# Start addresses of SBUF pools: two unused tiles and three tiles rounded up to 512 bytes

## The chip, the cores and the metric

The kernel runs on one core of one Trainium2 chip. The metric is the device time of one execution in microseconds, as the median of several runs. TensorE does the matrix products, VectorE (DVE) and ScalarE (ACT) the element-wise work, GpSimd (POOL) a little of it in the first third, and SyncE (SP) issues nearly all DMA transfers.

## The reference

Two layers of a diffusion backbone over 512 latent tokens of 1024 channels, with 256 context tokens. Layer 0 mixes the tokens with neighbourhood attention and a bidirectional gated recurrence, layer 1 with a gated short convolution; each layer ends in a gated feed-forward stage with a convolution of three taps. All in float32:

```
h = modulate(rms_norm(x, norm_mix_w[l]), shift_m, scale_m)
y = even_mixer(h, h_ctx, ...) if l == 0 else short_conv_mixer(h, ...)
x = x + gate_m * y
h = modulate(rms_norm(x, norm_ffn_w[l]), shift_f, scale_f)
a, val = split(h @ w_up[l])                  # 1024 -> 2 x 2816
x = x + gate_f * ((gelu(dwconv3(a)) * val) @ w_down[l])
...
return rms_norm(x, final_norm_w)
```

The six modulation vectors of a layer are `silu(c) @ ada_w[l] + ada_b[l]`.

## The kernel before

Activations stand transposed, 128 channels in the partitions and 512 tokens in the row. Each float32 operand is split into a high part (rounded to fp32r by a cast on ScalarE) and a low part (the difference, by VectorE), and a product is made of three matmuls, high by high, high by low and low by high: `mm3` (L287 to L290), and L1339 to L1341 in the last projection. The first argument after the output is the stationary operand (128 columns, 512 bytes in a partition), the next one the moving operand (256 or 512 columns).

Where the operands lie:

- `wp` holds the weights: two raw buffers `wraw` that DMAs fill, three pairs `whi`/`wlo` of 4096 bytes each, and `ws3`. In most stages `whi` and `wlo` are the stationary operands. In the value projection (L577) and in the last projection (L1339) they are the moving ones.
- `yp` holds the normalized activations of a stage (h, hf, hm: eight tiles of 4096 bytes, high and low part). They are the moving operands of most projections and the stationary ones of the value projection.
- `gq`, `zp` and `gp` hold the 22 gated feed-forward tiles g (a high and a low part each): g0 to g5 in `gq`, g6 to g9 in `zp`, g10 to g21 in `gp` (`gtiles`, L1216). They are the moving operands of the first down projection (pbd) and the stationary ones of the second (pd). At the ends of projections three weight pairs are put into `gq` too ("spare", L1050).
- `fp` holds the tiles T2 to T4 (sums of quarters of the activations, moving operands in the loop `group`, L1151), the results R and t of that loop, and small tiles, `ss` (L1333) among them.
- `np_` holds the attention tiles. The scores (L870) are made of QS (stationary) and KS (moving).
- `ap_` holds the rows of `ada_w` and their sums, and `ared` (L507).
- `xp` holds the residual stream xT.

The feed-forward stage takes most of the time: one `quad` (four output tiles of 128 channels, matmuls of 256 columns) and ten rounds of `group`, with matmuls of 256 columns on quarters of the product (p<-hf, p<-T) and of 512 columns on the rest (p<-hf). The stages follow each other in the written order; weights are loaded and split some calls ahead (`Weights.ahead`, L130).

Pools are stacked. Those of the left side begin where the one before them ends, from low addresses upward, in the order in which they are entered: cp, wp, ap_, zp, yp, and after them mp and later gp; kvp, hp and np_ come and go above. Those of the right side (xp, fp, gq) are stacked from the end of the partition downward. Every tile is rounded up to 32 bytes. So the size of a small tile in one pool sets where every later pool of its side begins.

Of the kernel before, what the change touches and what calls it, by code (L numbers as in the profile page):

```python
# [9 lines left out]
F32 = mybir.dt.float32  # L10
# [4 lines left out]
ALU = mybir.AluOpType  # L15
AX = mybir.AxisListType
PSUM = bass.MemoryType.PSUM

P = 128
# [155 lines left out]
def backbone(ctx: ExitStack, tc: tile.TileContext, a, out, dump=None):  # L175
    nc = tc.nc
    V, S, G, TE = nc.vector, nc.scalar, nc.gpsimd, nc.tensor
# [12 lines left out]
    cp = ctx.enter_context(tc.tile_pool(name="cp", bufs=1))  # L190
    wp = ctx.enter_context(tc.tile_pool(name="wp", bufs=2))
    ap_ = ctx.enter_context(tc.tile_pool(name="ap_", bufs=1))
# [52 lines left out]
    ident, sel = cst[:, 0:128], cst[:, 128:256]  # L245
# [11 lines left out]
    oml = cp.tile([P, 8], F32, name="oml")  # L257
    noml = cp.tile([P, 8], F32, name="noml")
    amul = cp.tile([P, 5, KT], F32, name="amul")
    rowv = lambda i, n: pv[:, i : i + n]  # L260


# [211 lines left out]
    class Ada:  # L474
# [3 lines left out]
        n, calls, raw, late = 0, 0, {}, []  # L478
# [9 lines left out]
        def unit(self, aux):  # L488
            self.calls += 1
            while self.late and self.late[0][0] <= self.calls:  # L490
                self.late.pop(0)[1]()
            if self.n >= 8 * len(self.jobs):
                return
            r = self.n % 8
            l, p_, j = self.jobs[self.n // 8]
            while len(self.raw) < min(self.n + 3, 8 * len(self.jobs)):
                self.load()
            raw = self.raw[self.n]
            self.n += 1
            if r == 0:  # L500
                self.acc = ap_.tile([P, T], F32, tag="aacc", name=f"aa{self.n}", bufs=1)
                pin(V.tensor_scalar(self.acc[:], raw[:], sil[:, 0, 0:1], None, ALU.mult))
                return
            pin(V.scalar_tensor_tensor(self.acc[:], raw[:], sil[:, r, 0:1], self.acc[:], ALU.mult, ALU.add))  # L504
            if r < 7:
                return
            red = ap_.tile([P, 16], F32, tag="ared", name=f"ad{self.n}", bufs=1)  # L507
            V.tensor_reduce(red[:], self.acc[:].rearrange("p (b j) -> p b j", j=32), axis=AX.X, op=ALU.add,
                            apply_transpose=True)
            pm = []  # L510

            def gather():
                pm.append(aux(f"pad{l}{p_}{j}"))
                TE.matmul(pm[0][:, 0:16], sel, red[:], start=True, stop=True)

            def finish():
                c = p_ * 8 + 4 * j
                for qd in range(4):
                    s4 = slice(32 * qd, 32 * qd + 32)
                    V.tensor_tensor(mod[s4, l, c : c + 4], pm[0][s4, qd:16:4], abT[s4, l * 48 + c : l * 48 + c + 4],  # L520
                                    ALU.add)
                if p_ in (1, 4):
                    w0 = (16 if p_ == 1 else 32) + 8 * l + 4 * j
                    V.scalar_tensor_tensor(amul[:, 2 * l + (1 if p_ == 1 else 2), 4 * j : 4 * j + 4], mod[:, l, c : c + 4],
                                           1.0, pv[:, w0 : w0 + 4], ALU.add, ALU.mult)

            self.late += [(self.calls + 3, gather), (self.calls + 5, finish)]

    ada = Ada()
# [440 lines left out]
                wv.tick()  # L970


    xp = ctx.enter_context(tc.tile_pool(name="xp", bufs=1, side="right", reuse_waits="tile"))
    xT = [xp.tile([P, T], F32, name=f"xT{k}") for k in range(KT)]
    for k in range(KT):
        nc.sync.dma_start(xT[k][:], x[k * P : (k + 1) * P, :])
    fp = ctx.enter_context(tc.tile_pool(name="fp", bufs=1, side="right", reuse_waits="tile"))
# [349 lines left out]
    for i in range(4):  # L1327
        for k2 in range(2):
# [1 line left out]
            for k in range(4):  # L1330
                TE.transpose(pt[:, k * P : (k + 1) * P], xT[4 * k2 + k][:, i * P : (i + 1) * P], ident)
            S.copy(xk[i][:, k2 * T : (k2 + 1) * T], pt[:])
    ss = fp.tile([P, 4, 8], F32, tag="ss", name="ssf")  # L1333

    def down(o, w, i, k0):
        ts = slice(i * P, (i + 1) * P)
# [91 lines left out]
```

## Time and profile before

| | |
|---|---|
| median of 3 runs | 1334.43 us (1333.52 to 1336.91) |
| the profiled execution | 1333.99 us, its span 1332.2 us |
| granted clock of TensorE, mean | 0.995 |
| TensorE matmul busy | 1304.5 us, 8456 matmuls |
| VectorE, ScalarE busy | 965.4 us, 625.2 us |
| bytes moved | 172.35 MB, mean 129 GB/s |

In the rows of the timeline the first number is the start in us from the beginning of the span, the second the duration of the row, then engine, line, operation, output and inputs by their names in the program, and how many instructions the row merges. In the rows of the groups the numbers behind the bar are the busy time in us and the mean duration in ns of one, then the idle time of the engine just before them with what ended it. In the rows of the waits they are us in total, times, and the longest. In a row of the windows the numbers are the stretch, its length, and the busy time and count of instructions of PE, PEld, DVE, ACT and POOL.

### The profile page before, as it was taken

To read this page: it belongs to the slowest core of one execution; us is meant where nothing else is said; L and a number is where in the kernel's file an instruction comes from. 1 tells how busy PE (TensorE), PEld (TensorE's weight loads), DVE (VectorE), ACT (ScalarE), POOL (GpSimd) and SP (SyncE) were. 2 spreads that over 40 slices of the span, in tenths; PEclk is the share of its full clock that TensorE was granted. 3 is DMA by queue.
4 is the path that set the end of the run, shared out by engine and by line. 5 is a ranking of instruction groups with operands and counts; after the bars stand their busy time and mean duration, and the time that the engine had idled before them with its cause. 6 is when DMAs were issued, how large, how long until landed. Compare 5 with 4: busy or idle time off the path is not lost. (4 is left out here: it accounts for less than half of the span.)

```text
span 1332.2 us, 21229 instructions
## 1 busy us (share of the span) xinstructions
PE 1304.5 (98%) x8456; PEld 1147.6 (86%) x8456; DVE 965.4 (72%) x1688; ACT 625.2 (47%) x1085; POOL 84.3 (6%) x87
## 2 busy tenths in 40 slices
PE   7999999999999999999999999999999999999997
PEld 4798888888779998889877898888999989899997
DVE  4668897887778878788766776667789897782333
ACT  4443445555545656565422253223456565663223
POOL 2204332311000000000000000000000000000000
PEclk9999999999999999999999999999999999999999
DMA  9842113674562122323466734555403423242231
GB/s 293 265 123 84 33 33 82 152 182 134 153 206 96 64 99 92 127 71 119 141 211 198 226 132 143 167 165 174 158 27 117 142 80 127 80 146 69 91 108 64
DMA packets 134995, 172.35 MB, mean 129 GB/s; under 512 B 14320, under 2 KB 103792, under 8 KB 129776
## 3 DMA queue, kind: packets, MB, share of 16 engines
q1 hardware_dynamic: 132896, 166.15, 39.3%
q10 hardware_dynamic: 2000, 4.85, 1.4%
q8 instruction: 66, 1.08, 0.3%
q14 instruction: 33, 0.27, 0.1%
HBM read 165.21 MB, written 2.10 MB: 126 GB/s over the span
## 5 line engine op out<-in xcount | busy, mean ns | idle before, releaser
L92 ACT CAST whi<-wraw 128x1024 fp32r<-128x1024 f32 (+1 forms) x122 | 124.1, 1021 | 280.8 <-PE pd L1340 70.4
L93 DVE TENSOR_TENSOR wlo<-wraw,whi 128x1024 fp32r<-128x1024 f32 (+1 forms) x122 | 145.2, 1192 | 107.7 <-ACT whi L92 107.1
L288 PE MATMUL p<-hf,whi 128*128 128x512 f32 (+1 forms) x640 | 215.4, 338 | 1.4 <-ACT whi L125 1.4
L290 PE MATMUL p<-hf,wlo 128*128 128x512 f32 (+1 forms) x640 | 214.6, 335 | 0.0
L289 PE MATMUL p<-hf,whi 128*128 128x512 f32 (+1 forms) x640 | 214.1, 335 | 0.0
L125 ACT CAST whi<-wraw 128x512 fp32r<-128x512 f32 (+1 forms) x160 | 113.0, 727 | 85.0 <-PE p L289 35.0
L290 PEld LDWEIGHTS p<-hf,wlo 128*128 128x128 f32 x640 | 120.1, 188 | 13.6
L288 PEld LDWEIGHTS p<-hf,whi 128*128 128x128 f32 x640 | 120.1, 188 | 12.3 <-ACT whi L125 1.6
L289 PEld LDWEIGHTS p<-hf,whi 128*128 128x128 f32 x640 | 120.1, 188 | 10.7
L126 DVE TENSOR_TENSOR wlo<-wraw,whi 128x512 fp32r<-128x512 f32 (+1 forms) x160 | 128.1, 817 | 0.9 <-ACT whi L125 0.5
L504 DVE SCALAR_TENSOR_TENSOR aa<-ar,sil,aa 128x512 f32<-128x512 f32 x140 | 104.8, 749 | 24.1 <-DMA ar<-in_ada_w_dram 21.8
L1339 PE MATMUL pd<-whi,g 128*128 128x256 f32 x352 | 98.2, 279 | 0.0
L1341 PE MATMUL pd<-wlo,g 128*128 128x256 f32 x352 | 98.1, 279 | 0.0
L1340 PE MATMUL pd<-whi,g 128*128 128x256 f32 x352 | 97.9, 278 | 0.0
L288 PE MATMUL pbd<-g,whi 128*128 128x512 f32 (+1 forms) x192 | 73.5, 383 | 0.0
L289 PE MATMUL pbd<-g,whi 128*128 128x512 f32 (+1 forms) x192 | 73.3, 382 | 0.0
L290 PE MATMUL pbd<-g,wlo 128*128 128x512 f32 (+1 forms) x192 | 73.1, 381 | 0.0
L288 PE MATMUL p<-T,whi 128*128 128x256 f32 x240 | 69.0, 288 | 0.0
L290 PE MATMUL p<-T,wlo 128*128 128x256 f32 x240 | 67.2, 280 | 0.0
L289 PE MATMUL p<-T,whi 128*128 128x256 f32 x240 | 67.2, 280 | 0.0
L1340 PEld LDWEIGHTS pd<-whi,g 128*128 128x128 f32 x352 | 66.3, 188 | 0.0
L1339 PEld LDWEIGHTS pd<-whi,g 128*128 128x128 f32 x352 | 66.1, 188 | 0.0
(679 smaller groups left out, 3296.3 us busy)
## 6 DMA issues: line engine op xcount, KB each, us to landing
ar<-in_ada_w_dram SPq DMA_DIRECT2D x160, 256.0 KB, 3.1
wraw<-in_upq_dram SPq DMA_DIRECT2D x40, 1024.0 KB, 4.8
wraw<-in_ffn_w_down_dram SPq DMA_DIRECT2D x16, 1024.0 KB, 5.3
wraw<-in_od_w_in_dram SPq DMA_DIRECT2D x12, 1024.0 KB, 5.6
wraw<-in_ev_w_in_dram SPq DMA_DIRECT2D x20, 512.0 KB, 5.2
araw<-in_ada_w_dram SPq DMA_DIRECT2D x16, 512.0 KB, 6.3
wraw<-in_ffn_w_down_dram SPq DMA_DIRECT2D x8, 768.0 KB, 4.7
wraw<-in_ev_w_out_dram SPq DMA_DIRECT2D x4, 1024.0 KB, 6.9
```

The costliest lines, as they stand in the source:

```text
L92: self.nc.scalar.copy(hv, rv)
L93: self.pin(self.nc.vector.tensor_tensor(lv, rv, hv.bitcast(F32), ALU.subtract))
L125: self.nc.scalar.copy(hi, src)
L126: V.tensor_tensor(lo, src, hi.bitcast(F32), ALU.subtract)
L288: TE.matmul(o, wh, mh, start=start, stop=False, skip_group_check=True)
L289: TE.matmul(o, wh, ml, start=False, stop=False, skip_group_check=True)
L290: TE.matmul(o, wl, mh, start=False, stop=stop, skip_group_check=True)
L504: pin(V.scalar_tensor_tensor(self.acc[:], raw[:], sil[:, r, 0:1], self.acc[:], ALU.mult, ALU.add))
L1339: TE.matmul(o[i][:, 0:256], gh[:, ts], w[0][:, k - k0], start=k == 0, stop=False)
L1340: TE.matmul(o[i][:, 0:256], gl[:, ts], w[0][:, k - k0], start=False, stop=False)
L1341: TE.matmul(o[i][:, 0:256], gh[:, ts], w[1][:, k - k0], start=False, stop=k == FT - 1)
```

## The change

Two tiles that nothing reads or writes are added, and three small tiles are made larger:

```diff
+    cp.tile([P, 144], F32, name="even")
...
-            red = ap_.tile([P, 16], F32, tag="ared", name=f"ad{self.n}", bufs=1)
-            V.tensor_reduce(red[:], self.acc[:].rearrange("p (b j) -> p b j", j=32), axis=AX.X, op=ALU.add,
+            red = ap_.tile([P, P], F32, tag="ared", name=f"ad{self.n}", bufs=1)[:, 0:16]
+            V.tensor_reduce(red, self.acc[:].rearrange("p (b j) -> p b j", j=32), axis=AX.X, op=ALU.add,
                             apply_transpose=True)
...
-                TE.matmul(pm[0][:, 0:16], sel, red[:], start=True, stop=True)
+                TE.matmul(pm[0][:, 0:16], sel, red, start=True, stop=True)
...
+    ep = ctx.enter_context(tc.tile_pool(name="ep", bufs=1, side="right"))
+    ep.tile([P, 120], F32, name="even2")
     xp = ctx.enter_context(tc.tile_pool(name="xp", bufs=1, side="right", reuse_waits="tile"))
...
-    ss = fp.tile([P, 4, 8], F32, tag="ss", name="ssf")
+    ss = fp.tile([P, P], F32, tag="ss", name="ssf")[:, 0:32].rearrange("p (i n) -> p i n", n=8)
```

The unused tile in `cp` has 576 bytes a partition and fills that pool up to a multiple of 512; the one in the new pool `ep`, 480 bytes, lies between `xp` and the right end of the partition. `ared` grows from 64 to 512 bytes and `ss` from 128 to 512. What follows for the first byte of each pool in a partition, from the allocation of the two built programs:

| pool | before | modulo 512 | now | modulo 512 |
|---|---|---|---|---|
| wp | 9152 | 448 | 9728 | 0 |
| ap_ | 52160 | 448 | 52736 | 0 |
| zp | 60416 | 0 | 61440 | 0 |
| yp | 76800 | 0 | 77824 | 0 |
| mp, gp | 109568 | 0 | 110592 | 0 |
| hp, np_ | 150528 | 0 | 151552 | 0 |
| gq | 160608 | 352 | 159744 | 0 |
| fp | 185184 | 352 | 184320 | 0 |
| xp | 212960 | 480 | 212480 | 0 |

The tiles of wp, gq, fp (T, R, t) and xp are multiples of 512 bytes long, and the slices of 128 columns that become stationary are 512 bytes long, so within these pools all operands of matmuls share the start of the pool modulo 512. KS and QS lie at 0 modulo 512 before and now. The weights of the very first projection (w0h, w0l) lie at 96 before and now. All instructions, their order on each engine and what they wait for are the same in both programs.

## The prediction

> **What bounds the kernel now.** I read the page first: the span, the busy shares, the slices.
>
> ```profile
> span 1332.2 us, 21229 instructions
> ...
> PE 1304.5 (98%) x8456; PEld 1147.6 (86%) x8456; DVE 965.4 (72%) x1688; ACT 625.2 (47%) x1085; POOL 84.3 (6%) x87
> ...
> PE   7999999999999999999999999999999999999997
> ...
> PEclk9999999999999999999999999999999999999999
> ```
>
> TensorE is busy in 98% of the span and in 9 tenths or more of every slice but the first and the last, at the full granted clock throughout. No other engine comes near. The waits say the same from the other side:
>
> ```profile
> PE prx L412 <- ACT sqx L410: 5.1, 1, 5.1
> ...
> PE p L288 <- ACT whi L125: 1.4, 2, 0.7
> ...
> ACT whi L92 <- PE pd L1340: 70.4, 18, 4.8
> ```
>
> The longest wait of TensorE for anybody is 5.1 us, once, at the start (L412); in the whole feed-forward loop (L288) it waits 1.4 us. ScalarE waits 70.4 us for TensorE, because a weight buffer comes free only when the last matmul that reads it is done. So the time is the number of matmuls times the step from one matmul's start to the next, and a change that adds no work can act only through this step. These groups hold most of the matmuls (each of them is one of a triple of lines with equal counts):
>
> ```profile
> L288 PE MATMUL p<-hf,whi 128*128 128x512 f32 x320 | 125.7, 393 | 0.0
> L1339 PE MATMUL pd<-whi,g 128*128 128x256 f32 x352 | 98.2, 279 | 0.0
> L288 PE MATMUL p<-hf,whi 128*128 128x256 f32 x320 | 90.1, 283 | 1.4 <-ACT whi L125 1.4
> L288 PE MATMUL p<-T,whi 128*128 128x256 f32 x240 | 69.0, 288 | 0.0
> L288 PE MATMUL pbd<-g,whi 128*128 128x512 f32 x160 | 64.3, 402 | 0.0
> ```
>
> The mean durations (279 to 402 ns) overlap, so they are not the step. The step is read in the timeline, from the starts of the first and the last matmul of an undisturbed run and the number of steps between them.
>
> **The step depends on where operands start.** Each matmul has a stationary operand, loaded while the matmul before it streams, and a moving operand. I write m/s for their start bytes modulo 512, m of the matmul that streams and s of the weights being loaded beside it, as the allocation of the built program gives them. First the last stage (L1339 to L1341), where one line, one shape and one set of moving tiles (m 448) meets stationary tiles of two pools: g6 to g21 at 0, then g0 to g5 at 352.
>
> ```profile
> 1275.18 0.28 PE L1339 MATMUL pd<-whi,g 128*128 128x256 f32 x1
> ...
> 1293.88 0.28 PE L1339 MATMUL pd<-whi,g 128*128 128x256 f32 x1
> ...
> 1295.17 0.28 PE L1341 MATMUL pd<-wlo,g 128*128 128x256 f32 x1
> ...
> 1300.21 0.28 PE L1341 MATMUL pd<-wlo,g 128*128 128x256 f32 x1
> ```
>
> 448/0: 165 steps in 18.70 us, 113.3 ns each. 448/352: 42 steps in 5.04 us, 120.0 ns. The same instructions on the same engine, 6.7 ns apart, so the start byte matters. The other classes with 256 columns, hf against whi (0/448) and T against whi (352/448), and one more of 0/448 in the first projection of the feed-forward stage:
>
> ```profile
> 463.15 0.28 PE L288 MATMUL p<-hf,whi 128*128 128x256 f32 x1
> ...
> 465.98 0.28 PE L288 MATMUL p<-hf,whi 128*128 128x256 f32 x1
> ```
>
> ```profile
> 453.19 0.28 PE L289 MATMUL p<-T,whi 128*128 128x256 f32 x1
> ...
> 454.00 0.28 PE L290 MATMUL p<-T,wlo 128*128 128x256 f32 x1
> ```
>
> ```profile
> 422.01 0.28 PE L289 MATMUL ppa<-hf,whi 128*128 128x256 f32 x1
> ...
> 422.46 0.28 PE L290 MATMUL ppa<-hf,wlo 128*128 128x256 f32 x1
> ```
>
> These are 24 steps of 117.8 ns, 7 of 117.1 and 4 of 113.3. The 0/448 class has two rhythms, 113.3 and about 117.8; over the dense part it averages 116.8. With 512 columns (0/448, then 352/448, then 0/96 in the first projection):
>
> ```profile
> 818.25 0.39 PE L288 MATMUL ppc<-hm,whi 128*128 128x512 f32 x1
> ...
> 849.84 0.39 PE L288 MATMUL ppb<-hm,whi 128*128 128x512 f32 x1
> ```
>
> ```profile
> 652.92 0.40 PE L290 MATMUL pbd<-g,wlo 128*128 128x512 f32 x1
> ...
> 660.42 0.40 PE L289 MATMUL pbd<-g,whi 128*128 128x512 f32 x1
> ```
>
> ```profile
> 61.58 0.40 PE L290 MATMUL pq<-h,w0l 128*128 128x512 f32 x1
> ...
> 64.86 0.40 PE L289 MATMUL pq<-h,w0h 128*128 128x512 f32 x1
> ```
>
> 138 steps of 228.9 ns, 32 of 234.3, 14 of 234.3. The last two share neither start; they share the difference s minus m, which is 96 in both. That is my first reason to think that the distance of the two streams counts, and not each start by itself.
>
> **What the change makes.** It adds, removes and moves no instruction: on every engine the built program has the same instructions in the same order with the same waits, SP's and POOL's queues included. It moves starts: weights (wp) from 448 to 0, g0 to g5 and spare weights (gq) and the T tiles (fp) from 352 to 0; the tiles at 0 stay at 0. So nearly every matmul becomes 0/0. The kernel has this class already in one place, the attention scores, KS against QS, both at 0:
>
> ```profile
> 276.85 1.00 PE L870 MATMUL ps<-KS,QS 128*128 128x256 f32 x7
> ```
>
> ```profile
> 313.96 1.00 PE L870 MATMUL ps<-KS,QS 128*128 128x256 f32 x7
> ```
>
> ```profile
> 242.05 0.40 PE L290 MATMUL pk<-h,wlo 128*128 128x512 f32 x1
> 242.28 0.28 PE L870 MATMUL ps<-KS,QS 128*128 128x256 f32 x1
> ```
>
> In the first two rows seven matmuls take 1.00 us with the last one's 0.28 us: 6 steps in 0.72 us, 120 ns, as slow as 448/352 though both operands are on 512. The last two rows are a 512-wide matmul at 0 beside which the first QS at 0 is loaded: 236 ns to the next start, where the three steps before it are 230, 231 and 226. There are seven such places, 231 to 236 ns.
>
> So I take 120 ns for 256 columns at 0/0. Its bounds are 113.3 ns (the best class) and 125 ns (the longest single step in the score rows). For 512 columns the bounds are 226.6 ns (twice 113.3) and 236; I take 232.5, halfway between the 229 of 0/448 and 236, since a single place is no steady run.
>
> After 418 us, where TensorE has no waits worth naming, the classes count as follows (matmuls, mean step now, to which step, sum). 256 columns: 0/448 1342 from 116.8 to 120, +4.3 us; 352/448 720 from 117.7, +1.7; 0/352 382 from 117.5, +1.0; 448/0 768 from 113.4, +5.1; 448/352 276 at 120.0, 0. 512 columns: 0/448 1907 from 229.1 to 232.5, +6.5; 352/448 143 from 234.1, -0.2. Sum +18.4 us, all on the path. Before 418 us the same sum is +5.3 us (604 of 512 columns, 745 of 256; the 128 of 0/96 keep their starts), but there TensorE does wait:
>
> ```profile
> 100.00:200.00 100.00, 96.30 (x730) 83.52 (x730) 88.93 (x150) 43.85 (x73) 36.56 (x38) 1.00 0.18 49
> ```
>
> With 3.7 us idle and VectorE at 88.9 in this stretch, I count half, +2.6 us. The other engines gain or lose nothing by their starts:
>
> ```profile
> L284 ACT CAST T<-df x6: 620/622/624, 435.8 to 982.2; 128x512 fp32r<-128x512 f32 x6
> ...
> L284 ACT CAST mgh<-gg x4: 607/616/622, 156.7 to 367.9; 128x512 fp32r<-128x512 f32 x4
> ```
>
> ```profile
> L285 DVE TENSOR_TENSOR T<-df,T x6: 676/690/693, 436.7 to 982.9; 128x512 fp32r<-128x512 f32 x6
> ...
> L285 DVE TENSOR_TENSOR mgl<-gg,mgh x4: 682/688/693, 175.4 to 368.5; 128x512 fp32r<-128x512 f32 x4
> ```
>
> T lies at 352 and mgh, mgl, gg at 0: 622 against 616 ns, 690 against 688. The ared and ss tiles, rounded up, feed 20 small reductions and the last four scalings; they are read and written in the same shapes, so I cost them at nothing. DMAs land at new starts (wraw from 448 to 0). No row has a landing with the start alone changed; they run beside TensorE, except in the first 45 us, and I leave them at zero.
>
> Sum: the profiled execution took 1333.99 us (span 1332.2); plus 18.4 and 2.6 is 1355.0. Its distance to the median of 1334.43 is 0.4 us, which is nothing here.
>
> **The rivals.** First, each start counts by itself, and 0 is the best for weights. For it: 113.3 against 120.0 in the last stage, where only the stationary tile's start differs, and the steadiness of 448/0 over 165 steps. Against it: KS and QS, both at 0, at 120 ns; and 0/448 at 113.3 in the first projection, where weights at 448 cost nothing. By it all go to 113.3 and 226.6. In the order above the dense classes give -4.7, -3.2, -1.6, -0.1, -1.8, -4.8 and -1.1, sum -17.3 us; before 418 us half of -3.3. That is 1315 us: faster. It decides if a weight load at 0 beside a moving operand at 0 runs at 113.3 in the group loop (L1151), where most of the matmuls are.
>
> Second, no change: the step is set by the rhythm in which matmuls follow each other, as the two rhythms of 0/448 suggest, and the classes trade gains (gq, T) for losses (448/0): 1334 us, give or take 4. The Trainium skill stands on this side. "SBUF — State Buffer", section "Who interferes with whom", gives the PE two independent SBUF read ports, one for the moving operand and one for weight loads, and says that PE never waits on anyone. Its section "Specifications (TRN2)" gives lines of 16 bytes and a penalty for crossing into a new one; all starts here are multiples of 32, before and after. By both sections the change would do nothing, and the time would stay at 1334 us. The trace speaks against it: 113.3 and 120.0 ns for one line and one shape.
>
> **How the numbers follow.** Slower as worked out, 0.56: two separate places of class 0/0 (KS with QS, and h with QS) are slow, and equal differences gave equal steps. Its own range is 1345 (512 columns stay at 229, and some of the 256 keep 117.8) to 1366 (512 columns at 236, early part counted in full). Faster, 0.32: the clean pair in the last stage is the best controlled row there is, and score runs are at most 8 matmuls long. No change, 0.12. A measurement of this kernel tells about 0.3%, 4 us, from nothing. The range goes from 1315, the full gain of the first rival, to 1366, and leaves out some 15 in 100: gains above that sum, and losses above the bounds.
>
> **What would show it.** In the changed kernel the timeline of the last stage, between about 1290 and 1310 us, would show steps of 120 ns for all g tiles, with the break between g5 and g6 gone; 113.3 there would make the first rival right, and the forecast's +5.1 us wrong first. The group loop's 256-wide triples would go to 120, the 512-wide runs to 230 or more; steps of 226.6 there would make the forecast wrong by twice the term. The granted clock and the idle time of TensorE should stay. If the steps are as now in all three places, the second rival holds.

## The result and the profile after

The changed kernel took **1342.53 us** (median of 4 runs, 1340.81 to 1344.33), the kernel before 1334.18 (4 runs): a ratio of 1.0059, with a 95% interval of 1.0039 to 1.0079. It is slower, as forecast, by 8 us where 21 were forecast. Both profiled executions are compared below: 1342.5 us of span against 1332.2. The profiled run of the changed kernel is the slowest of its four, so the traces differ by 10.3 us and the medians by 8.4. All times compared here are of executions at a granted clock of 0.99 or more; one of the twelve of T384_g352 below ran at 0.654, took 1828.86 us and is left out.

The page of the changed kernel, its span, busy times and the clock in 40 slices:

```profile
span 1342.5 us, 21229 instructions
...
PE 1314.5 (98%) x8456; PEld 1162.0 (87%) x8456; DVE 964.6 (72%) x1688; ACT 625.0 (47%) x1085; POOL 84.2 (6%) x87
...
PEclk8999999999999999999998999999999999999999
```

TensorE is busy 10.0 us longer with as many matmuls; VectorE and ScalarE have the times they had (965.4 and 625.2 before). So the loss is in the step of the matmuls, as the prediction had it. Three matmuls that both programs have in the same place of the sequence divide it. The timeline before (start, duration, engine, line, operation), then after:

```profile
407.82 0.28 PE L290 MATMUL pbo<-mgh,wlo 128*128 128x256 f32 x1
...
1208.12 0.28 PE L1340 MATMUL pd<-whi,g 128*128 128x256 f32 x1
...
1324.85 0.28 PE L1341 MATMUL pd<-wlo,g 128*128 128x256 f32 x1
```

```profile
410.40 0.28 PE L291 MATMUL pbo<-mgh,wlo 128*128 128x256 f32 x1
...
1213.79 0.28 PE L1343 MATMUL pd<-whi,g 128*128 128x256 f32 x1
...
1335.58 0.28 PE L1344 MATMUL pd<-wlo,g 128*128 128x256 f32 x1
```

The changed kernel is 2.6 us late at the first, 5.7 at the second and 10.7 at the third:

| stretch | forecast, us | measured, us |
|---|---|---|
| up to 408 | +2.6 | +2.6 |
| 408 to 1208 | +13.3 (256 columns +7.0, 512 columns +6.3) | +3.1 (256 columns +5.6, 512 columns -3.6, the rest +1.1) |
| last stage | +5.1 | +5.1 |

The last column sums the steps of the same matmul in both traces by class, from 418 us on (the ten before add nothing); the rest are some 200 steps longer than 140 ns (256 columns) or 260 ns (512 columns) in one of the traces, which hold a wait or a dip of the clock. That the first row agrees is luck. The prediction had taken half of a sum of +5.3 us, of which its 604 matmuls of 512 columns at +3.4 ns are +2.1 (an estimate from its own numbers) and those of 256 columns the other +3.2. By class the traces have +2.9 with 256 columns, nearly the whole, and -0.3 with 512. The steps are read as in the prediction, from first and last starts. The last stage and a run of T in the group loop, both 256 columns, in the changed kernel:

```profile
1290.10 0.28 PE L1343 MATMUL pd<-whi,g 128*128 128x256 f32 x1
...
1293.94 0.28 PE L1342 MATMUL pd<-whi,g 128*128 128x256 f32 x1
```

```profile
456.74 0.28 PE L291 MATMUL p<-T,wlo 128*128 128x256 f32 x1
...
460.70 0.28 PE L291 MATMUL p<-T,wlo 128*128 128x256 f32 x1
```

32 steps in 3.84 us and 33 in 3.96: 120.0 ns in both, the value taken for 0/0. Now a long run of 512 columns:

```profile
823.10 0.39 PE L291 MATMUL ppc<-hm,wlo 128*128 128x512 f32 x1
...
854.83 0.39 PE L290 MATMUL ppb<-hm,whi 128*128 128x512 f32 x1
```

140 steps in 31.73 us: 226.7 ns, where 232.5 was taken, and less than the 228.9 of 0/448 before. With 512 columns the new starts are the better ones: over all steps from 418 to 1208 us that are not longer than 260 ns the mean went from 229.4 to 227.7 ns.

### The profile page after: what moved, and what is told of

Read it like the earlier page. It is cut to its first block, busy times and chain, and to the rows that moved or that the text cites. A ratio compares the mean times of both kernels' runs of the same rounds, so it can differ in the third digit from the quotient of the medians.

```text
span 1342.5 us, 21229 instructions
## 1 busy us (share of the span) xinstructions
PE 1314.5 (98%) x8456; PEld 1162.0 (87%) x8456; DVE 964.6 (72%) x1688; ACT 625.0 (47%) x1085; POOL 84.2 (6%) x87
## 4 chain that ended last, share of the span: by engine, by line
PE 85%; DVE 8%; ACT 3%; DMA 2%; issue 1%; SPq 0%; ACTq 0%; DVEq 0%
PE p L289 11%; PE p L290 10%; PE p L291 10%; PE pd L1342 3%; PE pd L1344 3%; PE pd L1343 3%; PE pbo L289 2%; PE pbo L291 2%; PE pbo L290 2%; PE pbd L291 2%; PE pbd L289 2%; PE pbd L290 2%; DMA ar<-in_ada_w_dram 2%; PE ppc L289 1%; PE ppc L291 1%; PE ppc L290 1%
## 5 line engine op out<-in xcount | busy, mean ns | idle before, releaser
L290 PEld LDWEIGHTS p<-hf,whi 128*128 128x128 f32 x640 | 121.5, 190 | 10.3
L1342 PE MATMUL pd<-whi,g 128*128 128x256 f32 x352 | 100.0, 284 | 0.0
L1343 PE MATMUL pd<-whi,g 128*128 128x256 f32 x352 | 99.9, 284 | 0.0
L1343 PEld LDWEIGHTS pd<-whi,g 128*128 128x128 f32 x352 | 67.6, 192 | 0.0
L1342 PEld LDWEIGHTS pd<-whi,g 128*128 128x128 f32 x352 | 67.6, 192 | 0.0
```

Of the source, the lines that this page charges most:

```text
L290: TE.matmul(o, wh, ml, start=False, stop=False, skip_group_check=True)
L1342: TE.matmul(o[i][:, 0:256], gh[:, ts], w[0][:, k - k0], start=k == 0, stop=False)
L1343: TE.matmul(o[i][:, 0:256], gl[:, ts], w[0][:, k - k0], start=False, stop=False)
```

## The experiments

**The steps by themselves.** Two kernels measure nothing but the step, on 16 moving and 16 stationary tiles; 16 matmuls of each pair in a row, all pairs twice. Their body in place of the whole computation (512 in place of 256 in the second):

```diff
+    for r, (i, j) in enumerate(runs):
+        x, w, p = ms[offs[i]], ws[offs[j]], o[r % 8]
+        for k in range(16):
+            TE.matmul(p[:, 0:256], w[:, 128 * (k % 4) : 128 * (k % 4) + 128], x[:, 256 * (k % 2) : 256 * (k % 2) + 256],
+                      start=k == 0, stop=k == 15)
```

> This kernel leaves the whole computation out: it zeroes sixteen moving tiles (ma to mp, starting at 0, 32, ... 480 modulo 512) and sixteen stationary tiles (wa to wp, the same starts), and runs each of the 256 pairs twice as 16 matmuls with 256 columns in a row, in two different orders. Theory A, the step depends on the distance s minus m alone: equal steps along every diagonal, near 120 ns for distance 0, 113.3 for 64, 117 to 118 for 96, 352 and 448, 120 for 416, whatever the starts. Theory B, each start counts by itself: the table splits into rows or columns, for instance every moving tile at 448 (mo) at 113.3 or every moving tile at 0 (ma) at 117 to 120 whatever the weights. Theory C, the rhythm with which a run is entered decides: the two passes of one pair differ by several ns, without order in the table.

> The same kernel with 512 columns; the computation is left out here too. Theory A: equal steps along diagonals: 226.7 ns for distance 0, about 229 for 448, 234 for 96. Theory B: rows or columns, moving tiles at 352 slow (234), at 0 fast with weights at 0 (226.7) and slow with weights at 96 (234). Theory C: the two passes differ, 226.7 in one and 231 to 236 in the other for the same pair.

Here the timeline joins a run into one row; its duration less that of the last matmul (0.28 or 0.39 us) over 15 is the mean step. With 256 columns (ma, me, mh, mi, mo start at 0, 128, 224, 256, 448, and so do the w tiles):

```profile
162.57 2.08 PE L204 MATMUL og<-mo,wo 128*128 128x256 f32 x16
...
264.57 2.08 PE L204 MATMUL oe<-me,we 128*128 128x256 f32 x16
...
272.12 2.08 PE L204 MATMUL oa<-mi,wa 128*128 128x256 f32 x16
...
464.77 2.01 PE L204 MATMUL og<-mo,wa 128*128 128x256 f32 x16
...
481.77 2.05 PE L204 MATMUL oh<-mh,wa 128*128 128x256 f32 x16
...
828.26 2.05 PE L204 MATMUL og<-mo,wa 128*128 128x256 f32 x16
```

Three pairs with other starts but a distance of 0 or 256 all take 120 ns a step. The pair 448/0 (mo, wa) takes 115 ns the first time and 118 the second. With 512 columns (mc at 64, wi at 256, wl at 352, wo at 448):

```profile
149.64 3.83 PE L204 MATMUL oc<-mc,wa 128*128 128x512 f32 x16
...
379.80 3.83 PE L204 MATMUL oa<-ma,wo 128*128 128x512 f32 x16
...
498.62 3.81 PE L204 MATMUL oa<-ma,wi 128*128 128x512 f32 x16
...
513.40 3.82 PE L204 MATMUL oe<-me,we 128*128 128x512 f32 x16
...
914.18 3.90 PE L204 MATMUL oa<-ma,wl 128*128 128x512 f32 x16
```

Distance 192 (64/0 and 0/448) and distance 0 take 228 to 229 ns, distance 96 takes 234. From the last twelve steps of each run, by the distance s minus m modulo 256 (medians of the two passes):

| distance | 256 columns, ns | 512 columns, ns |
|---|---|---|
| 0 | 120.1, 120.0 | 228.4, 228.4 |
| 32 | 117.9, 118.1 | 233.2, 232.8 |
| 64 | 113.8, 117.8 | 233.7, 233.3 |
| 96 | 117.1, 118.3 | 234.4, 234.3 |
| 128 | 118.3, 118.9 | 232.6, 233.0 |
| 160 | 120.0, 120.0 | 233.7, 233.3 |
| 192 | 117.8, 117.8 | 228.9, 228.9 |
| 224 | 117.8, 116.7 | 233.3, 233.3 |

Theory A holds: pairs of one distance agree within 2 ns in a pass, whatever their starts, except at 64 and 256 columns, where two values occur (113.3 to 113.8, and 117.8), at 96 and 256 columns (117.1 to 120.0), and for the first runs of a kernel (one with 512 columns, two with 256), where the steps are still 427 and 213 ns. The 228.4 of distance 0 is no settled step: in the second pass the fourth to the seventh step of such a run are some 236, 228, 233 and 231 ns, and the last eight 226 to 227. The distance counts modulo 256, not 512. Theory B falls: there is no good row or column. Theory C holds in so far as one pair of distance 64 takes either value, and in small part one of 96. But the class before is not what decides. In the second pass sixteen runs of distance 64 follow each other, so that all but the first come after the same class:

```profile
561.83 2.05 PE L204 MATMUL ob<-mb,wl 128*128 128x256 f32 x16
563.71 2.05 PE L204 MATMUL oc<-mc,wm 128*128 128x256 f32 x16
565.60 2.00 PE L204 MATMUL od<-md,wn 128*128 128x256 f32 x16
567.44 2.05 PE L204 MATMUL oe<-me,wo 128*128 128x256 f32 x16
569.33 2.05 PE L204 MATMUL of<-mf,wp 128*128 128x256 f32 x16
571.22 2.00 PE L204 MATMUL og<-mg,wa 128*128 128x256 f32 x16
```

Every third run settles at 113.3 ns and the two between at 117.8, in both such rows of sixteen. An order of this kind looks like a phase that is carried from run to run; no run here tests that.

**The change taken apart.** One kernel has only the left side of the change (weights from 448 to 0):

```diff
+    cp.tile([P, 144], F32, name="even")
...
+            red = ap_.tile([P, P], F32, tag="ared", name=f"ad{self.n}", bufs=1)[:, 0:16]
```

> The left side of the change alone (the unused tile in cp and the longer ared): weights go from 448 to 0, gq and fp stay at 352, xp at 480. By the steps that the two traces show: 0/448 to 0/0 gives +4.4 us with 256 columns and -3.3 with 512, 448/0 to 0/0 gives +7.0, 448/352 to 0/352 gives -0.7. 352/448 to 352/0 is a class not seen (720 with 256 columns between 113.3 and 120, 143 with 512 between 226.7 and 236): -4.2 to +1.9, taken as 0. Sum +7.4, so 1341.6 us (1337.4 to 1343.5). If the loss does not come from the steps but from landings of the DMAs or the other engines on the right side, this one stays at 1334.

1342.51 us, 1.0056 of before (1.0036 to 1.0075): the whole loss. The class that had not been seen, T at 352 with weights at 0, in the timeline of this kernel:

```profile
456.78 0.28 PE L289 MATMUL p<-T,whi 128*128 128x256 f32 x1
...
458.22 0.28 PE L289 MATMUL p<-hf,whi 128*128 128x256 f32 x1
```

12 steps in 1.44 us, 120 ns: distance 160 in the table. The other has only the right side:

```diff
+    ep = ctx.enter_context(tc.tile_pool(name="ep", bufs=1, side="right"))
+    ep.tile([P, 120], F32, name="even2")
...
+    ss = fp.tile([P, P], F32, tag="ss", name="ssf")[:, 0:32].rearrange("p (i n) -> p i n", n=8)
```

> The right side of the change alone (the pool ep and the longer ss): gq, fp and xp go to 0, the weights stay at 448. By the steps: 0/352 to 0/0 +0.9 us, 352/448 to 0/448 -0.6 with 256 columns and -0.7 with 512, 448/352 to 448/0 -1.8. Sum -2.2, so 1332.0 us: slightly faster than before, less than can be told. If the right side carries the loss, 1342.

1330.29 us, 0.9967 (0.9954 to 0.9980): faster than before (the profiled run, 1335.32 us, is the slowest of its twelve). T, now at distance 192 as hf is, gained more than expected (117.7 to 115.0 ns), and hf beside it too (117.7 to 115.2 ns). But the last stage lost: the pair 448/0, at 113.3 ns before, ran at 117.8 in this kernel with every start in it unchanged:

```profile
1211.72 0.28 PE L1341 MATMUL pd<-whi,g 128*128 128x256 f32 x1
...
1309.95 0.28 PE L1341 MATMUL pd<-whi,g 128*128 128x256 f32 x1
```

834 steps in 98.23 us. So distance 64 has two rhythms here too, and something other than the starts chooses.

**What chooses the rhythm.** One kernel runs eight distances with 256 and 512 columns, 24 matmuls each, and enters each class once from every other:

```diff
+    for r, c in enumerate(path):
+        w, p, n = ws[c % 8], o[r % 8], 256 * (1 + c // 8)
+        for k in range(24):
+            TE.matmul(p[:, 0:n], w[:, 128 * (k % 4) : 128 * (k % 4) + 128], m[:, 512 * (k % 2) : 512 * (k % 2) + n],
+                      start=k == 0, stop=k == 23)
```

> The computation is left out: one moving tile at 0 and eight stationary tiles at 0, 32, ... 224, matmuls with 256 and with 512 columns, so sixteen classes, each run 24 matmuls long and entered once from each of the other fifteen. Theory D, the distance sets which rhythms are possible, and where there are two, the run before decides which: with 256 columns and distance 64 the step is 113.3 to 113.8 ns after some classes (after distance 0 for certain, from the first grid) and 117.8 after others, and it stays so for the whole run; distance 0 gives 120 after every class. With 512 columns distance 0 gives 226.7 and distance 192 gives 228.9 at the end of the run, after every class. Rival, the absolute start or chance decides: the steps of distance 64 show no order by the class before, or change within a run.

Rows of its timeline (wa, wc, wd, we at distances 0, 64, 96, 128):

```profile
463.10 5.77 PE L207 MATMUL of<-m,wd 128*128 128x512 f32 x24
468.71 2.99 PE L207 MATMUL og<-m,wc 128*128 128x256 f32 x24
...
908.53 3.01 PE L207 MATMUL og<-m,we 128*128 128x256 f32 x24
911.38 2.89 PE L207 MATMUL oh<-m,wc 128*128 128x256 f32 x24
914.10 3.04 PE L207 MATMUL oa<-m,wa 128*128 128x256 f32 x24
```

Over 23 steps, wc takes 117.8 ns after distance 96 with 512 columns and 113.5 after distance 128 with 256. A run keeps its rhythm to the end: 117.8 or 113.3 in its last twelve steps. Distance 192 does the same (113.3 after three of the fifteen classes, 117.8 after the others). Distance 0 has 120.0 ns at the end after 14 of the 15 (120.3 after one). With 512 columns distance 0 ends at 226.7 after every class, distance 192 at 228.9 after 13 of 15 (233.3 after two). But distance 64 took 117.8 here after distance 0, where the first pass of the grid had 113.3 to 113.8: theory D falls here too, the class before does not decide.

Three kernels then set the right side apart from the left: T (fp) at 0 or 384 and g0 to g5 (gq) at 352 or 448, weights at 448 throughout. The first, beside the pool ep and the longer ss (T384_g352 has 8 in place of 40 and the short ss of before, T0_g448 has 16):

```diff
+    eq = ctx.enter_context(tc.tile_pool(name="eq", bufs=1, side="right"))
+    eq.tile([P, 40], F32, name="even3")
```

> Weights at 448 as before, the T tiles (fp) at 0, g0 to g5 and the spare weights (gq) at 352 as before. Theory D: the T tiles gain as in the run right (256 columns 117.7 to 115.0, -1.8 us; 512 columns -0.7; hf beside them -1.5 or so), and the last stage keeps 113.3 ns for g6 to g21, since it is entered from distance 160 as before: 1.0 to 4.0 us below before, and 2.8 us below right by the traces, so about 1327.5 to 1330. Rival: the last stage's 113.3 came from elsewhere in memory or time and not from the class before it; then it goes to 117.8 here too and the time is that of right, 1330 to 1332.

1332.75 us, 0.9984 (0.9974 to 0.9993): 2.9 us below the 1335.62 of before on that chip, inside the 1.0 to 4.0 that were expected, but not at the 1327.5 to 1330 that were named with them. The trace agrees with the expectation: last stage at 120.0 and 113.3 as before, T at 114.8.

> As the kernel before, but with the T tiles (fp) at 384, a distance of 64 to the weights at 448; gq stays at 352. Theory D with the fast rhythm: the 720 matmuls of T with 256 columns go from 117.7 to 113.3, -3.1 us, so 1331.3; with the slow rhythm of distance 64 (117.8), nothing, 1334.5. The 143 with 512 columns stay near 233. Rival, each start by itself: T at 384 gives whatever it gives with all weights, no 113.3.

1336.06 us, 1.0010 (0.9999 to 1.0021). T at distance 64 took 117.5 ns: the slower rhythm, nothing gained.

> As T0_g352, but with gq at 448, so that the last stage is entered from distance 0 (120 ns) and not 160. Theory D: g0 to g5 at 120.0, g6 to g21 at 113.3 to 113.8 after them, as after distance 0 in the grid: the time of T0_g352, 1327.5 to 1330. Rival: only distance 160 leads into the fast rhythm; then g6 to g21 stay at 117.8, +3.4 us, 1331 to 1333.

1336.07 us, 1.0010 (0.9998 to 1.0021). The rival's rhythm came, though not its time: g0 to g5 at 120.0 and g6 to g21 at 117.8 after them. Its last stage takes 3.4 us more than that of T0_g352; the spans differ by 6.2 us, and the rest was not followed up. In the timeline, a stretch of g6 to g21:

```profile
1277.38 0.28 PE L1343 MATMUL pd<-whi,g 128*128 128x256 f32 x1
...
1297.76 0.28 PE L1345 MATMUL pd<-wlo,g 128*128 128x256 f32 x1
```

173 steps in 20.38 us, 117.8 ns. Distance 0 ahead of distance 64 gave the slower rhythm here. That only distance 160 leads into the faster one, as the rival has it, does not hold either: entry reached it after seven of the fifteen classes.

**On one chip.** The changed kernel, right and T0_g352 once more, with a fourth that has gq at 384:

```diff
+    eq.tile([P, 32], F32, name="even3")
```

> The changed kernel once more, on the same chip as the next three. If the steps make the loss, 1.006 of before again (the interval of the first comparison was 1.0039 to 1.0079); if it was that chip's clock, within 0.3% of before.

> The right side alone once more: gq, fp and xp at 0, weights at 448. Its first comparison gave 0.9967, with granted clocks of 0.994 to 0.998 in its runs. The last stage in the slow rhythm (+2.8 us by the trace) should make it slower than T0_g352_b by some 3 us on the same chip at the same clock; if it is faster, the last stage is not where the two differ.

> T at 0, gq at 352, weights at 448 once more. By the traces 4.6 us less in the T and hf matmuls of the dense part than before and the last stage as before: 0.9965 to 0.9985 of before, and below right_b by some 3 us.

> As T0_g352, with gq at 384: g0 to g5 as stationary at a distance of 192 from the weights (117.8 or 113.3 ns by the table of entries, 120.0 at 352). The table has 113.3 for distance 64 after distance 192. Then the last stage gains 0.6 to 1.8 us on T0_g352, and the spare weights at a distance of 128 lose some 0.4: equal to T0_g352_b within 1.5 us. If the run before does not decide the rhythm alone (as T0_g448 showed for distance 0), the 768 of g6 to g21 may fall to 117.8: +3.4 us, about the time of right_b.

| kernel | median, us | ratio to before (1335.17) | interval |
|---|---|---|---|
| after_b | 1343.28 | 1.0056 | 1.0043 to 1.0069 |
| right_b | 1332.26 | 0.9978 | 0.9965 to 0.9990 |
| T0_g352_b | 1331.65 | 0.9974 | 0.9964 to 0.9985 |
| T0_g384 | 1332.11 | 0.9976 | 0.9967 to 0.9986 |

The loss of the change came again. The 3 us between right_b and T0_g352_b did not, and the one trace of right_b shows a reason. It is the same program as right, yet its last stage ran in the other rhythm:

```profile
1211.75 0.28 PE L1341 MATMUL pd<-whi,g 128*128 128x256 f32 x1
...
1309.90 0.28 PE L1343 MATMUL pd<-wlo,g 128*128 128x256 f32 x1
```

866 steps in 98.15 us, 113.3 ns, against 117.8 in right. So the rhythm of distance 64 can differ between two executions of one program. These two were on different chips, but the chip alone does not choose: at the start of the same stage, before matmuls of other lines (L1326 and L1333) come between, right_b has the slower rhythm too:

```profile
1199.05 0.28 PE L1342 MATMUL pd<-whi,g 128*128 128x256 f32 x1
...
1201.41 0.28 PE L1341 MATMUL pd<-whi,g 128*128 128x256 f32 x1
```

20 steps in 2.36 us, 118 ns, with the same starts. The rhythm is worth 4.5 us over the 1010 steps of that stage. T0_g384 had 113.3 in its last stage throughout, g0 to g5 included (distance 192). Right_b, T0_g352_b and T0_g384 keep the weights at 448 and put T at 0. Each is some 0.25% faster than before, and so faster than both kernels of this case; they can't be told from one another. The same is not true of every kernel with these starts: T0_g448 has them too, and with its last stage at 117.8 ns it was no faster than before (1.0010).

## Why the prediction was right and wrong

- **What bounds the kernel, and that only the step can change: right.** The busy time of TensorE grew by 10.0 us, the span by 10.3, and no other engine moved by more than 0.8.
- **The distance of the two starts counts, not each start: right**, by the grids, where all pairs at distance 0 take 120 ns. The distance goes by 256, not 512, which the prediction did not see, and with 256 columns it does not always fix the step: at distance 64 or 192 there are two. The first rival (0 is the best start for weights) falls: it built its 17 us of gain on the pair 448/0, whose distance is 64.
- **256 columns at 0/0 take 120 ns: right.** The last stage gave +5.1 us as forecast. Between 408 and 1208 us +5.6 came of +7.0: some matmuls at the entry of a run take 112 to 118 ns before 120 sets in.
- **512 columns at 0/0 take 232.5 ns: wrong, and this is the step that failed.** The term was +6.3 us (+6.5 and -0.2), after 418 us; it measured -3.6, the other way. The prediction's own range for the slower outcome, 1345 to 1366 us, began where these steps stay at 229, and so left out that they could gain. The 232.5 ns stood on seven single places, 231 to 236 ns, where h is followed by QS. The changed kernel shows what such a place is, at the start of a run of 512 columns after one of 256:

```profile
460.82 0.40 PE L289 MATMUL p<-hf,whi 128*128 128x512 f32 x1
...
462.21 0.39 PE L289 MATMUL p<-hf,whi 128*128 128x512 f32 x1
...
466.29 0.28 PE L289 MATMUL p<-hf,whi 128*128 128x256 f32 x1
```

The first 6 steps take 1.39 us, 231 ns each (single ones up to 235); the next 18 take 4.08 us, 226.7 each. After a change of class distance 0 begins slowly and then settles, here within six steps, in entry within ten. A single place, where the distance changes from 448 to 0 for one step, shows the beginning and not the rhythm. The settled step is the lower bound that the prediction gave, 226.6 ns: with it the two dense terms of 512 columns are -4.8 and -1.1 in place of +6.5 and -0.2, and the sum is 1342.8 us. That this meets the median so closely is in part luck: many runs of 512 columns are only 3 to 24 matmuls long and keep their slow start, so -3.6 came of these -5.9, while 256 columns gave less than forecast.

- **The other engines and the DMAs cost nothing: held.** Sums over the steps leave +1.1 us in long steps for waits and dips of the clock between 408 and 1208 us, and -0.1 before. The left side of the change alone made the whole loss, so the new starts of gq, fp and xp are not needed for it.
- **The second rival, no change, falls** with its reason: the Trainium skill's "SBUF — State Buffer" ("Who interferes with whom") has two independent ports for TensorE, and the steps here depend on where the two operands stand to one another (113.3 to 120.0 ns with 256 columns). What inside the chip joins them was not measured.

## What to carry to other kernels

Where TensorE is the bound and every matmul loads new weights, the distance between the starts of the moving and the stationary operand is worth up to 6% of a step, and rounding pools to one multiple sets that distance to 0 nearly everywhere: here the best for 512 columns and, with distance 160, the worst for 256. Read a step from a run that has settled, never from a single place between two classes. And before small offsets are tuned further, look whether two executions of one program agree in the stage in question.

## What was not expected of the hardware

- With 256 columns and distance 64 or 192 there are two stable rhythms, 113.3 and 117.8 ns, kept for up to 1010 matmuls; the same program took one in one execution and, on another chip, both in one execution. What chooses is open. Runs of right spread from 1327.65 to 1335.32 us; how much of that is rhythm and how much the granted clock (0.994 to 0.998 in these runs) stays open.
- Settled, 512 columns at distance 0 take twice the best step of 256 columns (226.7 and 113.3 ns), while 256 columns at distance 0 take the worst (120.0).
- The Trainium skill's "TensorE: Matmul & The Clock Gate", section "Back-to-back issue gap", gives N / 2.4 + 2.5 ns for an isolated matmul and about 131 ns for 512 columns in a stream with weight loads; the least settled step of fp32r read here with 512 columns is 226.7 ns, and for these kernels that is the number to go by.
